# A decoder trunk re-laid with a transposed residual, streamed weights, and feed-forward work interleaved with attention

## The chip, the cores and the metric

The kernel runs on all eight cores of one Trainium2 chip, two dies of four cores each. Every core computes one batch element of 4,096 tokens, and no core waits for another. The metric is device time in microseconds of the slowest core. Some executions fall into a second, slower state: the cores of one die, or of both, show a lower granted TensorE clock (the share of full speed at which TensorE is let run) and take some per cent longer (in one run of the old kernel, experiment 9, 19,823.8 us at 0.881 on one die beside 18,640.3 at 0.958 on the other). I compare fast runs with fast runs. In the later jobs I compare single cores on a die that shows no lower clock in its records, and I call that an undisturbed die.

## The reference

Four layers. Each has a half-step SwiGLU feed-forward, a mixer, and a second half-step feed-forward. The model width is 1,024 and the hidden width 2,816. The mixer has 6 differential heads (two 32-wide score components, causal), 6 forgetting heads (causal with a learnt decay) and 4 dilated heads (an exact mixture of three windows, 2,048 tokens back at most).

```python
def reference(x, w_in, ...):
    for l in range(DEPTH):
        x = x + 0.5 * swiglu(rms_norm(x, g_ffn1[l]), w1_gate[l], w1_up[l], w1_down[l])
        x = x + hybrid_mixer(rms_norm(x, g_mix[l]), w_in[l], ...)   # diff | forgetting | dilated, then @ w_o
        x = x + 0.5 * swiglu(rms_norm(x, g_ffn2[l]), w2_gate[l], w2_up[l], w2_down[l])
    return rms_norm(x, g_final)
```

## The kernel before

It runs in stages, layer by layer over all 4,096 tokens: feed-forward, projections, attention, output projection, feed-forward. A small recording layer gives each engine its instructions and adds the semaphore waits that the buffers need (a semaphore is a counter by which one engine tells another, or itself, that work is done). Weights of a stage stay on chip while the stage runs. The stages in order, cut:

```python
    for idx, l in enumerate(layers):
        phase_ffn(c, g, w["w1_gate"][l], ...)
        phase_proj(c, g, sc, w["w_in"][l], ...)
        phase_attn(c, g, sc, w["w_o"][l], ...)
        phase_ffn(c, g, w["w2_gate"][l], ...)
    phase_final(...)
```

In attention the loop is a pipeline over items of one 128-key block and 512 queries. Scores are made two items ahead (`PRE`), and values are taken two items late (`LAG`), so TensorE, ScalarE (the exponential) and TensorE again work on different items:

```python
        LAG = ATT_LAG        # 2
        PRE = ATT_PRE        # 2
        for i in range(min(PRE, len(items))):
            emit_S(items[i])
        for i, it in enumerate(items):
            ...
            c.op("act", lambda e: e.activation(out=p[:, col0:w1], in_=sbk[:, col0:w1], func=AF.Exp,
                                               scale=hd["scale"]), reads=SBKS, writes=[P])
            ...
            if i + PRE < len(items):
                emit_S(items[i + PRE])
            if i >= LAG:
                emit_PV(i - LAG)
```

The softmax here doesn't subtract the row's maximum and nothing guards it: scores larger than these inputs give would overflow.

## Time and profile before

The median was 19,086.98 us over three runs (19,032.48 to 19,121.04). The profiled execution's slowest core took 18,680.2 us.

| stretch of layer 0 | us | what is busy in it |
|---|---|---|
| first feed-forward | 984 | TensorE |
| projections | 580 | TensorE |
| attention | 1,780 | TensorE and ScalarE both about 91% |
| output projection | 152 | TensorE |

These lines are from the page of the kernel before: its span, busy time by engine, three rows of the 40 equal slices (a digit is a busy share in tenths; PEclk is the granted TensorE clock in tenths of full speed), and the chain of work that ended last.

```profile
span 18680.2 us, 262548 instructions; the slowest of 8 cores (18600.2 to 18680.2 us)
PE 16574.1 (89%) x75072; PEld 7111.5 (38%) x75072; DVE 6278.7 (34%) x7537; ACT 9004.0 (48%) x17109; POOL 929.4 (5%) x716
PE   8978999799997899979898889997989898998794
ACT  2214999422222599932221269992222227998121
PEclk9989999999998999999999999999999999999997
PE 80%; DMA 8%; ACT 4%; DVE 4%; issue 3%; another core or an unknown queue 1%; SPq 1%; POOL 0%; ACTq 0%; DVEq 0%; POOLq 0%
```

The four runs of nines in the ScalarE row are the four attention stages. Between them ScalarE is nearly idle. A busy ScalarE in attention and a nearly idle one in the feed-forward is what the change sets out to even out.

The next lines are the table by stretch of the same kernel: the window, its length, then busy time and instruction count of TensorE matmuls, weight loads, VectorE, ScalarE and GpSimd, then granted clock, DMA share and GB/s.

```profile
core 3: us, PE busy (x) PEld busy (x) DVE busy (x) ACT busy (x) POOL busy (x), PEclk, DMA share, GB/s
119.00:1103.00 984.00, 889.05 (x4287) 409.79 (x4285) 208.83 (x292) 235.76 (x369) 6.12 (x7) 0.96 0.25 60
1103.00:1683.00 580.00, 526.93 (x2504) 236.97 (x2502) 193.53 (x259) 117.92 (x222) 114.10 (x82) 0.96 0.27 83
1690.00:3470.00 1780.00, 1624.70 (x6768) 632.54 (x6768) 885.48 (x953) 1613.72 (x3233) 76.23 (x55) 0.98 0.09 17
3470.00:3622.00 152.00, 121.20 (x512) 46.40 (x512) 43.72 (x64) 0.00 (x0) 0.00 (x0) 0.99 0.70 213
```

Attention keeps both engines at about 91% (1,624.70 and 1,613.72 of 1,780). If attention's matmuls could be mixed with the feed-forward's, ScalarE would no longer set its pace.

### The profile page before, as it was taken

How to read it: one execution, taken by the hardware profiler on the slowest of the kernel's cores; microseconds unless marked ns; L12 is line 12 of the kernel's file. 1: busy time of each engine (PE TensorE's matmuls, PEld its weight loads, DVE VectorE, ACT ScalarE, POOL GpSimd, SP SyncE). 2: the span in 40 equal slices, each digit the busy share in tenths (PEclk: the TensorE clock that was granted, in tenths of full speed). 3: DMA queues.
4: the chain of work that ended last, by engine and by line, in shares of the span. 5: the costliest groups of instructions: out<-in, count | busy, mean ns of one | idle time of the engine just before them, and what ended most of it. 6: DMA issues, size and time to landing. Idle time of an engine off the chain costs nothing.

```text
span 18680.2 us, 262548 instructions; the slowest of 8 cores (18600.2 to 18680.2 us)
## 1 busy us (share of the span) xinstructions
PE 16574.1 (89%) x75072; PEld 7111.5 (38%) x75072; DVE 6278.7 (34%) x7537; ACT 9004.0 (48%) x17109; POOL 929.4 (5%) x716
## 2 busy tenths in 40 slices
PE   8978999799997899979898889997989898998794
PEld 3433333244443333334444333333444343333341
DVE  2223444422222444532221344452222234445221
ACT  2214999422222599932221269992222227998121
POOL 0011000000001100000000110000000010000000
PEclk9989999999998999999999999999999999999997
DMA  4132001513114200151412310005141221001512
GB/s 87 52 84 64 10 13 23 116 59 84 55 50 95 53 12 12 23 124 54 88 55 61 88 40 12 16 20 132 55 90 55 67 85 29 10 17 34 126 55 92
DMA packets 854125, 1072.66 MB, mean 57 GB/s; under 512 B 339288, under 2 KB 529048, under 8 KB 844568
## 3 DMA queue, kind: packets, MB, share of 16 engines
q1 hardware_dynamic: 680240, 883.83, 15.8%
q0 software_dynamic: 172544, 172.03, 6.8%
q8 instruction: 710, 11.63, 0.3%
q14 instruction: 631, 5.17, 0.1%
HBM read 908.30 MB, written 319.36 MB: 66 GB/s over the span
## 4 chain that ended last, share of the span: by engine, by line
PE 80%; DMA 8%; ACT 4%; DVE 4%; issue 3%; another core or an unknown queue 1%; SPq 1%; POOL 0%; ACTq 0%; DVEq 0%; POOLq 0%
PE ps L832 16%; PE pp L295 13%; PE pp L299 13%; PE ps L327 12%; PE pp L766 12%; PE pp L520 4%; PE pp L528 3%; PE ps L562 2%; PE pp L761 2%; DMA out<-L3m_xr 1%; DMA fin_xt<-out 1%; DMA out<-L1m_xr 1%; PE pp L763 1%; DMA out<-L2m_xr 1%
## 5 line engine op out<-in xcount | busy, mean ns | idle before, releaser
L832 PE MATMUL ps<-L1m_pt,L1m_va 128*128 128x512 bf16 (+3 forms) x3072 | 1117.8, 364 | 35.4 <-DVE L1m_pt L886 16.4
L832 PE MATMUL ps<-L2m_pt,L2m_va 128*128 128x512 bf16 (+3 forms) x3072 | 1117.0, 364 | 32.2 <-DVE L2m_pt L886 15.5
L832 PE MATMUL ps<-L0m_pt,L0m_va 128*128 128x512 bf16 (+3 forms) x3072 | 1115.8, 363 | 32.6 <-DVE L0m_pt L886 16.4
L832 PE MATMUL ps<-L3m_pt,L3m_va 128*128 128x512 bf16 (+3 forms) x3072 | 1111.1, 362 | 32.7 <-DVE L3m_pt L886 16.4
L880 ACT ACTIVATE L1m_pt<-pp 128x512 bf16<-128x512 f32 (+3 forms) x2208 | 1043.0, 576 | 60.6 <-PE pp L763 22.5
L880 ACT ACTIVATE L2m_pt<-pp 128x512 bf16<-128x512 f32 (+3 forms) x2208 | 1043.0, 576 | 58.8 <-PE pp L763 21.6
L880 ACT ACTIVATE L0m_pt<-pp 128x512 bf16<-128x512 f32 (+3 forms) x2208 | 1043.4, 576 | 57.7 <-PE pp L763 20.3
L880 ACT ACTIVATE L3m_pt<-pp 128x512 bf16<-128x512 f32 (+3 forms) x2208 | 1042.8, 576 | 57.3 <-PE pp L763 20.1
L766 PE MATMUL pp<-L2m_qz,L2m_ks 128*128 128x512 bf16 (+3 forms) x1824 | 679.9, 373 | 55.6 <-ACT L2m_pt L880 55.5
L766 PE MATMUL pp<-L0m_qz,L0m_ks 128*128 128x512 bf16 (+3 forms) x1824 | 678.5, 373 | 56.2 <-ACT L0m_pt L880 55.8
L766 PE MATMUL pp<-L1m_qz,L1m_ks 128*128 128x512 bf16 (+3 forms) x1824 | 678.8, 373 | 55.7 <-ACT L1m_pt L880 55.5
L766 PE MATMUL pp<-L3m_qz,L3m_ks 128*128 128x512 bf16 (+3 forms) x1824 | 677.9, 372 | 55.7 <-ACT L3m_pt L880 55.5
L832 PEld LDWEIGHTS ps<-L1m_pt,L1m_va 128*128 128x128 bf16 x3072 | 295.3, 96 | 694.6 <-issue 643.3
L832 PEld LDWEIGHTS ps<-L2m_pt,L2m_va 128*128 128x128 bf16 x3072 | 295.1, 96 | 692.5 <-issue 640.0
L832 PEld LDWEIGHTS ps<-L0m_pt,L0m_va 128*128 128x128 bf16 x3072 | 295.2, 96 | 689.6 <-issue 638.2
L832 PEld LDWEIGHTS ps<-L3m_pt,L3m_va 128*128 128x128 bf16 x3072 | 294.7, 96 | 682.3 <-issue 628.8
L876 ACT ACTIVATE L0m_pt<-pp,L0m_bq 128x512 bf16<-128x512 f32 (+1 forms) x864 | 472.9, 905 | 40.3 <-DVE L0m_bq L734 34.3
L876 ACT ACTIVATE L1m_pt<-pp,L1m_bq 128x512 bf16<-128x512 f32 (+1 forms) x864 | 474.1, 884 | 36.5 <-DVE L1m_bq L734 25.7
L876 ACT ACTIVATE L2m_pt<-pp,L2m_bq 128x512 bf16<-128x512 f32 (+1 forms) x864 | 473.2, 904 | 36.2 <-DVE L2m_bq L734 29.3
L876 ACT ACTIVATE L3m_pt<-pp,L3m_bq 128x512 bf16<-128x512 f32 (+1 forms) x864 | 471.8, 909 | 32.7 <-DVE L3m_bq L734 27.8
L302 ACT ACTIVATE L0c_sg<-pp 128x512 f32<-128x512 f32 x176 | 105.1, 597 | 678.1 <-PE pp L295 669.8
L302 ACT ACTIVATE L1c_sg<-pp 128x512 f32<-128x512 f32 x176 | 105.1, 597 | 677.9 <-PE pp L295 677.6
(547 smaller groups left out, 29103.9 us busy)
## 6 DMA issues: line engine op xcount, KB each, us to landing
L0a_xt<-x SPq DMA_DIRECT2D x32, 512.0 KB, 4.0
L0a_xr<-x SPq DMA_DIRECT2D x64, 256.0 KB, 2.9
out<-L0a_xr SPq DMA_DIRECT2D x64, 256.0 KB, 2.3
L0p_xt<-out SPq DMA_DIRECT2D x32, 512.0 KB, 4.1
L0m_xr<-out SPq DMA_DIRECT2D x64, 256.0 KB, 3.9
out<-L0m_xr SPq DMA_DIRECT2D x64, 256.0 KB, 4.2
L0c_xt<-out SPq DMA_DIRECT2D x32, 512.0 KB, 3.9
L0c_xr<-out SPq DMA_DIRECT2D x64, 256.0 KB, 2.9
```

The source lines that it names most:

```text
L295: (lambda e, kc=kc: e.matmul(pg[:], wg[:, kc, fc * 128:(fc + 1) * 128], xnT[b][:, kc, :], start=(kc == 0), stop=(kc == 7)))
L299: (lambda e, kc=kc: e.matmul(pu[:], wu[:, kc, fc * 128:(fc + 1) * 128], xnT[b][:, kc, :], start=(kc == 0), stop=(kc == 7)))
L302: c.op("act", lambda e: e.activation(out=sg[fc % 2][:], in_=pg[:], func=AF.Silu), reads=[PG], writes=[SG[fc % 2]])
L327: (lambda e, fc=fc: e.matmul(py[:], hT[:, fc, tt * 128:(tt + 1) * 128], wd[:, fc, dh * 512:(dh + 1) * 512], start=(fc == 0), stop=(fc == N ...
L520: (lambda e, kc=kc: e.matmul(pa[:], wq[:, kc, col:col + 128], xnT[b][:, kc, :], start=(kc == 0), stop=(kc == 7)))
L528: (lambda e, kc=kc: e.matmul(pb_[:], wq[:, kc, rcol:rcol + 128], xnT[b][:, kc, :], start=(kc == 0), stop=(kc == 7)))
L562: (lambda e, kc=kc: e.matmul(pv[:], xnT[b][:, kc, tt * 128:(tt + 1) * 128], wv[:, kc, hf * 512:(hf + 1) * 512], start=(kc == 0), stop=(kc ...
L761: lambda e: e.matmul(sbk[:, col0:512], kt[0:K, kb * 128:(kb + 1) * 128], qt[0:K, q0 + col0:q0 + 512], start=True, stop=False),
L766: c.op("pe", lambda e: e.matmul(sbk[:, col0:512], kt[0:K, kb * 128:(kb + 1) * 128], qt[0:K, q0 + col0:q0 + 512], start=True, stop=True), r ...
L832: c.op("pe", lambda e: e.matmul(obk[:, col0:512], va[vs][:, kb, :], p[:, col0:512], start=it["first"], stop=it["last"]), reads=[P, VA[vs]] ...
L876: c.op("act", lambda e: e.activation(out=p[:, col0:512], in_=sbk[:, col0:512], func=AF.Exp, scale=hd["scale"], bias=bq[bi][:, kb:kb + 1]), ...
L880: c.op("act", lambda e: e.activation(out=p[:, col0:w1], in_=sbk[:, col0:w1], func=AF.Exp, scale=hd["scale"]), reads=SBKS, writes=[P])
```

## The change

The kernel is rewritten. Its parts:

- The residual is kept transposed (model width on partitions), so no activations are transposed, and the work goes in blocks of 1,024 tokens. Sixteen block-layers of attention (4 layers times 4 blocks) are numbered `a = 0..15`.
- All the work of a block that is not attention (output projection, second feed-forward, first feed-forward of the next layer, projections) is one long generator, which I call a **chain**. There are 20. Chain `a + 3` is to run during attention of block `a`.
- Weights stream in 0.5 MB units through a ring of six, once per block instead of once per layer.
- Differential scores use four 32-row tiles of the array at once; exponentials are 1,024 columns wide.
- Attention has PSUM banks 0 to 5. Chains have the two others. (PSUM is the memory that holds TensorE's results, used here as eight banks; copying a finished bank out is called an eviction.)

The core of the diff, cut. Everything in it is added; `...` marks cuts, and the comments after `#` are mine:

```diff
+    def filler_step(self, force=False):          # next piece of a chain: 8 matmuls of 512 columns, about 1.73 us
+        ...
+        r = next(self.fill_gen)
+        ...
+        self.remF -= r                           # chain work still to be handed out
+        return r

+        self.filler_init()                       # sets self.remF = 0.0
+        ...
+        self.fill_limit = n - 2                  # n = 4: the prologue runs chains 0, 1, 2
+        while self.filler_step() is not None:
+            pass
+        self.tlbanks = [6, 7]
+        pend = None
+        ui = 0
+        RES = 12.0
+        for a in range(L * n):
+            tgt = a + n - 1
+            self.fill_limit = tgt
+            self.remF += self.tl_cost(tgt)       # this block's chain work, in us
+            ...
+            def fill(t):
+                ...
+                budget += t * max(0.0, self.remF - RES) / max(remA, 1e-9)
+                while budget > 0 and self.gap <= 0:
+                    r = self.filler_step()
+                    ...
+                    budget -= r
+            for st in steps:
+                self.emit_S(st)
+                ct = cost(st)
+                fill(ct / 2)
+                if pend is not None:
+                    self.emit_PV(pend)           # values of the step before: one step late
+                pend = st
+                fill(ct / 2)
+                remA -= ct
```

So between the score matmuls and the value matmuls of a step some chain pieces are put in: `remF` is the chain work left, `remA` the attention steps left, and their ratio spreads the one evenly over the other. A second way in is forced: where attention needs something that an unfinished chain makes, it runs chain pieces until that is there.

```diff
+            if self.nch <= ch["i"] or self.nq <= hd["i"]:     # in emit_S: keys or queries not there yet
+                self.filler_step(True)
+    def need_wo(self, a):                                     # before an attention output is overwritten
+        while self.wo_done < a:
+            self.filler_step(True)
```

## The prediction

> **What bounds the kernel now.** It runs in stages. Busy time by stretch (layer 0): feed-forward about 984 us, PE 935 busy, clock 0.97 to 1.00; projection about 580, PE 523; attention 1780, with ScalarE busy 1614 (91%); output projection 152; the gaps between stages 34 to 90 us each, clock near 0.5. In the timeline the feed-forward's 128x512 matmuls come 0.216 us apart, so feed-forward and projection sit at the TensorE rate. In attention one 512-column exponential costs about 0.58 us per item and TensorE is held to that: 3072 items x 0.58 = 1780. The span is 18,680 us; the timed median is about 400 us above it.
>
> **What the change does.** Attention of one block shares TensorE with the feed-forward and projections of the block three ahead; ScalarE's 1.6 ms per layer should hide under matmuls.
>
> - Removed: the rotated-weight projections (640 matmuls per layer, 138 us, 550 in all), the transposes, stage gaps (about 250 us per layer), zero-padded scores. The differential scores become four K=32 row tiles at once. [...] no trace here shows it yet. [...]
> - TensorE work left, counted from the instruction order at 0.216 us per 512 columns: feed-forward 7,290, projections and output 1,870, attention 3,960, fp32 norm sums 90: about 13,200 us.
> - ScalarE: wide 1024-column exponentials (0.94 to 1.0 us, extrapolated from 0.28 to 0.61 us for 128 to 512 columns) total about 5,500; tanh 840, squares 500, copies and table loads (1.28 us each) 1,100: about 8,000. VectorE about 7,000.
> - Added: weights are streamed four times as often (0.5 MB per unit, every 6.9 us at worst). Before loads 17.3 MB in 117 us, twice that rate; it should hide.
>
> **What TensorE will still wait for** (estimates): 52 norms, each a serial chain of add, square, GpSimd add, fp32 matmul, Ln with table load, Exp, multiply: 8 to 9 us, partly filled: 400 us. The feed-forward filler has only two PSUM banks; a gate bank needs tanh (0.60) plus a VectorE op (0.69), about 1.7 us with semaphores, against 1.73 us of matmuls, and queues behind 1 us exponentials: 0.3 us per gate/up pair, 420 us. Projection evictions 150; single-buffered differential scores in the longest blocks 150; accumulator evictions 150; start and tail 60. Total about 1,330, so a span of 14,500 and, with the same 400 us offset, 14,900 us.
>
> **Chances.** Predicted 14,900 us, 8 in 10 within 14,100 to 16,200. Faster by over 2%: 0.97; within: 0.02; slower: 0.01.
>
> **What would show the steps right or wrong.** Page after: TensorE above 90% busy in nearly all slices, ScalarE 50 to 60%, DMA four tenths. Four row-tiled score matmuls start almost together. The chain of waits mainly TensorE, with waits on the evictions of the two filler banks and on the norm chain.
>
> **What would make it wrong.** A lower granted clock: [...] This case's trace disagrees so far: all eight cores hold 1.0 in the feed-forward. [...] Bank or queue waits larger than 0.3 us per pair: each 0.1 us costs 140 us.

Where the text is marked, passages are cut whose figures no trace or run had shown: the time of a group of four row tiles with the 900 us that tiles without overlap would add, and what I wrote of a lower clock's cause with a time of about 17,000 us worked out from it. The sum was 13,200 us of TensorE work plus 1,330 of waits, so a span of 14,500, and 14,900 with the offset. The cut time of a group is no separate term of it, and the record does not say what a group of row tiles counts for within the 3,960 us of attention. (With a group put down as one matmul of 0.216 us, the changed kernel's columns come to 13,157 us in the account below.) The 1.0 that all eight cores hold is read from 4,700 to 5,600 us of the kernel before, a feed-forward of layer 1, where each core's mean is 1.00; over the first feed-forward core 3 has 0.96, as in the table above.

## The result, and the profile after

| | median us | lowest to highest | runs |
|---|---|---|---|
| before | 19,060.32 | 19,032.48 to 19,121.04 | 4 |
| after | 20,717.72 | 20,527.38 to 20,831.25 | 4 |

The ratio of fast runs is 1.0847 (95% interval 1.0784 to 1.0909): the changed kernel is slower. The ratio is the mean time of one kernel's fast runs over that of the other's of the same rounds, so it is not quite the ratio of the two medians. I had predicted 14,900 us, faster with a chance of 0.97.

The same parts of the page, for the changed kernel:

```profile
span 20525.9 us, 227698 instructions; the slowest of 8 cores (20482.2 to 20525.9 us)
PE 16631.8 (81%) x68016; PEld 5945.0 (29%) x68016; DVE 6932.5 (34%) x10341; ACT 8106.0 (39%) x10325; POOL 2165.3 (11%) x2496
PE   6877788788897978778788787977978888777878
ACT  1133543633514153462441416256153232646361
PEclk9978799798798979879889897987987989796879
PE 63%; ACT 12%; issue 11%; DVE 7%; DMA 4%; POOL 2%; SPq 0%; ACTq 0%; DVEq 0%; POOLq 0%
```

I had expected TensorE above 90% in nearly all slices. It is mostly at seven or eight tenths. ScalarE is no longer in four lumps, but it still swings between 1 and 6 tenths, which an even mixture would not do. The clock row falls to 7 again and again, where the old kernel held 8 or 9 up to the last slice. TensorE's share of the last chain fell from 80% to 63%, and ScalarE, VectorE and "issue" took its place.

The table by stretch of one block (`a = 2`: differential, forgetting, dilated heads) on core 6 of the changed kernel:

```profile
core 6: us, PE busy (x) PEld busy (x) DVE busy (x) ACT busy (x) POOL busy (x), PEclk, DMA share, GB/s
2501.00:3530.00 1029.00, 855.23 (x3715) 306.14 (x3716) 326.01 (x486) 366.09 (x474) 129.77 (x151) 0.91 0.37 79
3530.00:3718.00 188.00, 143.43 (x581) 55.65 (x579) 40.16 (x49) 145.88 (x156) 1.04 (x1) 0.92 0.15 43
3718.00:3895.00 177.00, 141.99 (x325) 38.42 (x323) 79.62 (x130) 84.68 (x106) 0.00 (x0) 0.50 0.12 35
```

The dilated stretch runs at a granted clock of 0.50 from end to end. "PE busy 141.99 of 177" there doesn't mean that TensorE had much to do: while the clock records say 0.5, dense matmuls of 512 columns come 0.43 us apart in this trace in place of 0.216, and the columns of these matmuls at full clock would have filled 64 us, a share of 0.36. VectorE and ScalarE are busy less than half of it. GpSimd, which starts the weight loads for the chains, does nothing at all.

Where are the chain's matmuls? The same three stretches, restricted to the chains' first main matmul line (columns: window, length, matmuls, weight loads, clock, DMA share, GB/s):

```profile
2501.00:3530.00 1029.00, 418.53 (x1680) 162.44 (x1680) 0.91 0.37 79
3530.00:3718.00 188.00, 0.00 (x0) 0.00 (x0) 0.92 0.15 43
3718.00:3895.00 177.00, 0.00 (x0) 0.00 (x0) 0.50 0.12 35
```

All 1,680 of them are in the differential stretch; the forgetting and the dilated heads get none. It is so in every block: in the whole trace of core 6 no chain matmul stands between two matmuls of forgetting or dilated heads. The interleaving that the change is about doesn't happen in two of the three kinds of heads. And inside the differential stretch it comes in long bursts rather than evenly, as the account of the bookkeeping below shows.

### An account of the span

To see what TensorE's span is made of, I split every start-to-start interval of matmuls in the trace into three parts: the time that the columns need at full clock (0.2158 us for 512 columns, the spacing seen where matmuls run densely), the surplus that the granted clock explains, and the rest, a stall. This is my own computation from the trace's records, not a view of the profile. How a pause is shared between clock and stall depends on the rule: a recheck with another rule gave 1,958 and 5,265 for the changed kernel, with a sum within 25 us of the one below. A group of four row-tiled score matmuls is put down as one matmul; what it takes beyond that stands among the stalls.

```
us per core                       span   columns at  lower    stalls  before first and
                                         full clock  clock            after last matmul
predicted                       14,500     13,200        0     1,330  (in the stalls)
after, core 6                   20,526     13,157    1,762     5,483      123
reset, core 1 (experiment 1)    17,467     13,134      641     3,558      133
 + no self-wait, core 4         16,657     13,134      523     2,878      122
 + values two steps late, c. 1  16,330     13,132      485     2,579      134
```

The work was predicted well (13,200 against 13,157). What failed is everything between: stalls were 5,483 instead of 1,330, and the clock cost 1,762 where I had put nothing. The largest stalls after the change, with the same items after the fixes of the experiments:

```
us of stall                                          after   reset   +no self  +lag 2
value matmul after a score matmul (forg., dilated)   1,529     893       839      431
chain after chain, same kind of matmul               1,161     427       209      198
differential score after a value matmul              1,133     381       479      469
differential value after a differential value          565     550         8       (small)
differential value after a differential score          409     254       262      261
```

### The profile page after: what moved, and what is told of

It is laid out like the page before. It is cut to its first block, busy times and chain, and to the rows that moved or that the text cites. A ratio compares the mean times of both kernels' runs of the same rounds, so it can differ in the third digit from the quotient of the medians.

```text
span 20525.9 us, 227698 instructions; the slowest of 8 cores (20482.2 to 20525.9 us)
## 1 busy us (share of the span) xinstructions
PE 16631.8 (81%) x68016; PEld 5945.0 (29%) x68016; DVE 6932.5 (34%) x10341; ACT 8106.0 (39%) x10325; POOL 2165.3 (11%) x2496
## 4 chain that ended last, share of the span: by engine, by line
PE 63%; ACT 12%; issue 11%; DVE 7%; DMA 4%; POOL 2%; SPq 0%; ACTq 0%; DVEq 0%; POOLq 0%
PE ps L520 24%; PE ps L549 14%; PE ps L948 6%; PE ps L960 6%; ACT pt L893 6%; PE pp L911 5%; ACT pt L921 4%; PE pp L883 3%; PE pp L520 2%; DVE xn L505 2%; DMA s_vd<-hT 2%; DMA s_qf<-hT 2%; ACT pt L925 1%; PE ps L713 1%; PE pp L549 1%
## 5 line engine op out<-in xcount | busy, mean ns | idle before, releaser
L520 PE MATMUL ps<-xn,ring 128*128 128x512 bf16 x24216 | 5830.3, 393 | 376.9 <-ACT hT L687 118.7
L893 ACT ACTIVATE pt<-pp 128x1024 bf16<-128x1024 f32 (+3 forms) x3456 | 3100.6, 949 | 1425.1 <-PE pp L883 1420.8
L520 PEld LDWEIGHTS ps<-xn,ring 128*128 128x128 bf16 x24216 | 2327.9, 100 | 3775.5 <-issue 1430.3
L960 PE MATMUL ps<-pt,vr 128*128 128x512 bf16 (+3 forms) x5376 | 2040.6, 454 | 1091.3 <-DVE dd L982 393.6
L948 PE MATMUL ps<-pt,vr 128*128 128x512 bf16 (+3 forms) x6912 | 2307.9, 421 | 494.4 <-DVE dd L982 217.4
L549 PE MATMUL ps<-hT,ring 128*128 128x512 bf16 x10296 | 2378.4, 378 | 140.0 <-DVE t L585 0.2
L911 PE MATMUL pp<-qr,kr 66*128 66x512 bf16 (+3 forms) x5376 | 2083.5, 463 | 0.6
L921 ACT ACTIVATE pt<-pp,ckm 128x1024 bf16<-128x1024 f32 (+7 forms) x1920 | 1812.0, 964 | 570.9 <-PE pp L911 395.3
L549 PEld LDWEIGHTS ps<-hT,ring 128*128 128x128 bf16 x10296 | 937.4, 97 | 1577.7 <-issue 586.2
L984 DVE RECIPROCAL dd<-dd 128x128 f32<-128x128 f32 x1408 | 1338.7, 951 | 119.2 <-DVE dd L984 3.2
L960 PEld LDWEIGHTS ps<-pt,vr 128*128 128x128 bf16 x5376 | 539.3, 101 | 2711.3 <-issue 2634.7
L948 PEld LDWEIGHTS ps<-pt,vr 128*128 128x128 bf16 x6912 | 451.4, 99 | 1942.7 <-issue 1899.7
```

Source lines behind the costliest of these rows:

```text
L520: fns = [(lambda e, k=k: e.matmul(p[0:m, :] if m != 128 else p, w[:, woff + k * m:woff + (k + 1) * m], self.xn[:, k, b * 512:(b + 1) * 512 ...
L549: fns.append(lambda e, w=w, o=o, ap=ap, q=q: e.matmul(p, w[:, o:o + 128], ap, start=(q == 0), stop=(q == nblk - 1)))
L893: c.op("act", lambda e: e.activation(out=v3(p[:], c0, 512), in_=v3(self.pp[m][:], c0, 512), func=AF.Exp, scale=SCALE_D), reads=self.PS[2 * ...
L911: fns.append(lambda e, a0=a0, a1=a1, tri=tri: e.matmul(pp[:, a0:a1], kr[0:66, kc:kc + 128], qr[0:66, a0:a1], start=True, stop=not tri))
L921: c.op("act", lambda e: e.activation(out=p[:, lo:hi], in_=pp[:, lo:hi], func=AF.Exp, scale=1.0, bias=self.ckm[par][:, kb, hd["h"]:hd["h"] ...
L948: c.group("pe", [(lambda e, cc=cc: e.matmul(self.pst[cc][:, c0:512], va, p[:, cc * 512 + c0:(cc + 1) * 512], start=(st["first"] and m == 0 ...
```

## Experiments

Letters stand for theories where they are used: C is the wait of TensorE on its own semaphore, E is the single step between scores and values, G is that the half clock comes from too little TensorE work (a guess from the 0.50 at a share of 0.36 above; experiment 7 does not show it).

### The main theory: a counter that starts at minus 943.5

`remF` is meant to hold the chain work still to be handed out. The prologue runs chains 0 to 2 through the same `filler_step`, which subtracts each piece, but nothing was added for them. So the main loop starts with `remF` at minus the cost of three chains. Replaying the bookkeeping while the kernel is built (no chip needed) prints, for the first line of each kernel, `remF` as block 11's cost is added, and for the others how many us of chain work were forced and how many were spread:

```
after    a 11 remF before -400.9 adds 570.2
         -1 forced 0 free 943.5          (prologue)
          0 forced 0 free 0
          1 forced 342.1 free 0
          2 forced 506.3 free 63.9
         13 forced 570.2 free 0
         15 forced 255.7 free 483.8      (the rest, after the last attention)
reset    a 11 remF before 12.1 adds 570.2
          0 forced 0 free 300.7
          1 forced 0 free 572.0
          2 forced 0 free 570.2
         15 forced 0 free 524.0
```

Most blocks start from -400.9 and add 570.2. So `remF` is positive at first, but far too small, and the forced pieces soon use it up: of 570 us only 62 to 67 are spread. In blocks 0 and 1 and after block 12 it is never positive. There the budget is `t * max(0, negative)`, nothing. All the chain work then arrives by the forced way, in a burst when attention comes to a head whose keys or outputs are not ready. The rival was that the interleaving is sound and the two filler banks and their evictions make the stalls, as my prediction had it.

### Experiment 1: reset the counter

```diff
         self.tlbanks = [6, 7]
+        self.remF = 0.0
         pend = None
```

> One line: the account of filler time still to be placed (remF) is set to zero after the first three feed-forward chains, which had driven it to -943 us. Theory A (the schedule was never interleaved: with the account negative the budget is zero, and the chains run only where attention is forced to wait for them): filler now spreads over differential, forgetting and dilated heads; the granted clock rises from 0.86 to 0.97 or more, the time falls from 20,700 to about 14,500 to 15,600 us. Theory B (the loss is in the parts themselves: two PSUM banks for the chains, row tiles that do not overlap, weight streaming[...]): time stays within 3% of 20,700[...].

The result was correct. The first profiled execution had one die in the slow state:

```profile
die 0 (median of its cores): 17455.5 us, clock 0.934
die 1 (median of its cores): 18426.6 us, clock 0.859
```

In the seven runs (17,468.04 to 19,467.87) the undisturbed dies took 17,428 to 17,476 us. In one run both dies were undisturbed, and it took 17,468.04 us. The kernel before, in the same rounds, had no run without a slow die (19,521.27 to 20,557.94), so there is no ratio of fast runs; its one undisturbed die took 18,668 to 18,694. Theory A's numbers were missed all the same: the clock rose to 0.934 and not to 0.97, and the time did not come down to 15,600 us; experiments 3 and 4 go on from there. One added line is worth 20,526 - 17,467 = 3,058 us on a core: 1,925 of stalls and 1,121 of clock. On undisturbed cores the changed kernel goes from 9.9% slower than the old one (20,526 over 18,680) to 6.6% faster (17,452 over 18,681, middles of those ranges).

The same restriction to the chain's matmul line, same block, after the reset (differential, forgetting, dilated):

```profile
2846.00:3400.00 554.00, 197.23 (x776) 73.05 (x777) 0.94 0.35 76
3400.00:3705.00 305.00, 151.89 (x632) 61.33 (x631) 0.98 0.33 68
3705.00:3961.00 256.00, 73.83 (x272) 26.85 (x272) 0.89 0.47 118
```

776 + 632 + 272 = 1,680, the same matmuls, now spread. The whole block takes 554 + 305 + 256 = 1,115 us instead of 1,394. The dilated stretch holds more work, is longer, and runs at 0.89 instead of 0.50.

### Experiment 2: reset, but spread only in the first two layers

```diff
+        self.remF = 0.0
...
-                budget += t * max(0.0, self.remF - RES) / max(remA, 1e-9)
+                budget += (a < 8) * t * max(0.0, self.remF - RES) / max(remA, 1e-9)
```

> As e1_reset, but the budget is zero again from layer 2 on, so layers 0 and 1 interleave and layers 2 and 3 do not. Theory A: blocks of layers 0 and 1 take as long as in e1_reset, blocks of layers 2 and 3 as long as in the changed kernel (about 1,250 and 1,600 us for the second and fourth kind of block), and the time lies between the two, near 17,500 to 18,500 us. Theory B: no difference between the layers.

Correct; 20,042.85 us, with both dies on a lower clock (about 0.82 and 0.81), so its total says nothing (17,500 to 18,500 was expected) and only blocks of the same kernel may be compared. These are the three stretches of the fourth block of layer 1, with spreading, and of the fourth block of layer 2, without, on core 1, restricted to the chains' first main matmul line as before:

```profile
8859.00:9570.00 711.00, 248.61 (x880) 89.09 (x880) 0.85 0.33 74
9570.00:9958.00 388.00, 126.34 (x528) 51.04 (x528) 0.94 0.28 61
9958.00:10206.00 248.00, 85.78 (x272) 30.03 (x272) 0.75 0.42 110
13229.00:14422.00 1193.00, 400.75 (x1680) 159.93 (x1680) 0.87 0.33 73
14422.00:14669.00 247.00, 0.00 (x0) 0.00 (x0) 0.94 0.14 42
14669.00:14847.00 178.00, 0.00 (x0) 0.00 (x0) 0.51 0.11 33
```

The first block took 711 + 388 + 248 = 1,347 us, the second 1,193 + 247 + 178 = 1,618 us (1,250 and 1,600 were expected). On the other cores the pairs lie between 1,354 and 1,421, and between 1,618 and 1,718. One kernel thus shows both behaviours, and the switch between them is the spreading alone. This also speaks against a slow chip or a slow state as the cause.

### Experiment 3: leave out TensorE's waits on its own semaphore

The recording layer makes an instruction wait for the last writer of each bank it writes. Where a second group accumulates into the same bank, the last writer is TensorE itself, so TensorE waits until its own earlier group is done (0.32 us each time in a differential value product, see below). All 68,016 matmul records on core 6 of the changed kernel start in the order of the program, and the results of experiments 3, 4 and 8 stayed right without the wait: it guards nothing here.

```diff
     def wait(self, e, s, v):
+        if e == "pe" and s == "c_pe":
+            return
```

> e1_reset, and TensorE no longer waits on its own semaphore (it runs in order [...]). Theory C (in the interleaved kernel a part of what is left is TensorE waiting for its own drain between two groups that accumulate into one bank: 550 us between the two halves of a differential value product, some of the 430 us inside the chains): span of an undisturbed core falls from 17,460 by 500 to 900 us, and the 0.32 us pauses between those halves go. Rival D (those pauses are row-tile switching or late weights): no change beyond 1%.

Correct (on top of the reset). Undisturbed dies: 16,657 to 16,707 us; one run without a slow die, 16,692.09. That is 811 us less than the reset (17,467 to 16,657). The reset was measured on another chip; the kernel before took 18,609 to 18,694 us on undisturbed dies of that one and 18,585 to 18,739 on this one, so I take the two as alike. One step shows it. The timeline of the changed kernel (start, duration, engine, source line, operation, count), four value matmuls of a differential step:

```profile
4300.52 0.40 PE L883 MATMUL pp<-qr,kr 32*128 32x512 bf16 x4 [1.06 <-ACT pt L893]
4300.85 1.35 PE L948 MATMUL ps<-pt,vr 128*128 128x512 bf16 x4
```

and the same four without the self-wait:

```profile
4201.46 1.03 PE L950 MATMUL ps<-pt,vr 128*128 128x512 bf16 x4
```

1.35 - 1.03 = 0.32 us, 1,737 times in the changed kernel: 565 us in the account, and 8 us with the wait left out. The chain's long accumulations gained as well (chain after chain, 427 to 209). The first line shows something else: four 32-row score matmuls of 512 columns took 0.40 us from start to end together, where a single matmul of that size is shown with 0.38. They run at once. But the next matmul starts 0.33 us after the first of the four, not 0.216: more on this below.

### Experiment 4: values two steps late

```diff
-        pend = None
+        pends = deque()
...
-                if pend is not None:
-                    self.emit_PV(pend)
-                pend = st
+                if len(pends) >= 2:
+                    self.emit_PV(pends.popleft())
+                pends.append(st)
```

> e3_noself, and the value products follow their scores by two steps instead of one. Theory E (TensorE's 890 us of waits at the forgetting and dilated value products are for the mask and the exponential of the step just before): they halve, span falls by a further 300 to 500 us. Rival F (they are for the eviction of the two accumulators): less than 150 us.

Correct (on top of both fixes). All six runs were slow ones (16,775.72 to 18,441.7); in four of them one die was undisturbed, at 16,329 to 16,387 us (in the profiled one, two of its cores show 0.8125 for 154 us). That is 327 us less than experiment 3, and the stall of values behind scores fell from 839 to 431. What it cures can be read in the dilated stretch of the changed kernel. This is its timeline (start, duration, engine, line, operation; in brackets the idle time before it and what ended that), with lines in between cut:

```profile
3821.96 1.02 ACT L925 ACTIVATE pt<-pp 128x1024 bf16<-128x1024 f32 x1 [0.90 <-DVE pt L928]
...
3822.14 1.01 PE L960 MATMUL ps<-pt,vr 128*128 128x512 bf16 x2 [0.33 <-DVE pt L928]
...
3822.94 1.06 PE L911 MATMUL pp<-qr,kr 66*128 66x512 bf16 x2
...
3824.16 1.02 ACT L925 ACTIVATE pt<-pp 128x1024 bf16<-128x1024 f32 x1 [1.17 <-PE pp L911]
...
3825.28 0.69 DVE L928 TENSOR_TENSOR pt<-pt,wt 128x1024 bf16<-128x1024 bf16 x1 [1.50 <-ACT pt L925]
3826.16 1.02 ACT L925 ACTIVATE pt<-pp 128x1024 bf16<-128x1024 f32 x1 [0.98 <-PE pp L911]
...
3826.23 1.01 PE L960 MATMUL ps<-pt,vr 128*128 128x512 bf16 x2 [0.22 <-PE pp L911]
```

Follow one step: values of an earlier step at 3822.14, then this step's scores at 3822.94, the exponential at 3824.16, the mask product at 3825.28, its values at 3826.23. That is 4.09 us for two steps, and no engine is full: it is a round of handovers. With chain pieces put in between, TensorE has something to do in the meantime; with a second step under way, the round counts for less. The old kernel had that second step (`LAG` 2, `PRE` 2), and its dilated heads held a clock of 0.99; that the second step is the reason was not tested on it.

This version is the best that I ran. On one chip and in the same rounds its undisturbed dies took about 16,350 us, the kernel before's 18,585 to 18,739: about 12% less. All six of its runs were below all seven of the kernel before (19,790.87 to 20,718.78, also all slow ones).

### Experiment 5: load a quarter of each weight unit

After the first six, only a quarter of each unit is loaded, so the result is wrong (relative error 1.16), but the program is otherwise that of experiment 1.

```diff
+        w = 2048 if self.uld <= RING else 512
-        self.c.dma("pool", ..., self.ring[:, s * 2048:(s + 1) * 2048], self.w["w_units"][l, u], ...)
+        self.c.dma("pool", ..., self.ring[:, s * 2048:s * 2048 + w], self.w["w_units"][l, u][:, 0:w], ...)
```

> e1_reset with three quarters of the weight stream left out after the first six units (wrong result on purpose; the ring keeps old weights). The prediction said that the stream hides: then the span of an undisturbed core stays within 1.5% of 17,460 us and the stalls of TensorE within 200 us of 3,560. If the stream crowds out other transfers, the span falls by more than 500 us.

Its undisturbed die took 17,259 to 17,278 us, 1.1% less than experiment 1 on the other chip, with stalls of 3,409 against 3,558. In its two other runs both dies were slow. So the fourfold weight traffic is nearly hidden, as predicted, and is not where the time went. This run differs from experiment 1 in its chip and in the data of its weights too; what of the 1.1% belongs to the traffic was not separated.

### Experiment 6: the reset again, on the other chip

> The same kernel as e1_reset, as the reference of this chip: 17,460 us on an undisturbed die, more on a die whose clock is limited; stalls of TensorE near 3,560 us in either.

19,267.8 us, both dies on a lower clock (0.81 and 0.82). On core 4 the account gives 2,514 us to the clock, some 1,860 of them at 0.8125, and 3,194 to stalls, where I had expected 3,560 on any clock. This run is no measure of the reset: it shows what the lower clock cost this kernel.

### Experiment 7: dilated scores twice, in the changed kernel

```diff
+            if kind == "dil":
+                fns = fns + fns
             c.group("pe", fns, reads=[KR, QR, self.CONST], writes=PPS)
```

> The changed kernel without the reset of the counter; every score matmul of the dilated heads is issued twice in a row into the same banks (the second overwrites the first with the same values, so the result stays right). In the changed kernel the dilated stretches have no chain work and TensorE has about 64 us of full-clock work in 177 us (share 0.36) at a granted clock of 0.50 to 0.51; in the stretch that was looked at ScalarE and VectorE are busy less than half of it. Theory G (the half clock is granted because TensorE has little work there): the share of issued work rises to about 0.5 to 0.55, the granted clock in the dilated stretches rises clearly above 0.51 (0.7 or more), and the stretch does not get longer than 190 us although it holds about 30 us more work at full clock; the whole run stays within 1.5% of the changed kernel on cores of an undisturbed die. Rival (the half clock belongs to the data or to the shape of the dilated heads' matmuls): the clock stays at 0.50 and the stretches lengthen by about twice the added work, 50 to 70 us each, so the run by some 600 to 850 us.

Correct. The dilated stretch of block 2 on two cores of the undisturbed die, core 1 and core 3:

```profile
3753.00:3948.00 195.00, 169.19 (x483) 57.17 (x481) 79.89 (x130) 84.86 (x107) 0.01 (x1) 0.62 0.11 32
3756.00:3967.00 211.00, 196.01 (x486) 63.12 (x483) 79.50 (x130) 84.67 (x106) 0.00 (x0) 0.50 0.10 29
```

Neither expectation was met. On core 1 the stretch got 18 us longer (177 to 195) for 32 us more work at full clock, and the clock rose from 0.50 to 0.62, not to 0.7 or more. On core 3 the same stretch stayed at 0.50 and got 34 us longer, so 0.62 is no fair sample. Over the dilated stretches of core 1 (blocks 0 to 14) the share of work rose from 0.35 to 0.45 and the mean clock only from 0.51 to 0.54; on the die's other cores the mean was 0.54 to 0.56. Core 1's whole time rose by 301 us (20,827 against 20,526), at the upper edge of what theory G allowed and well under the rival's 600 to 850. In the two other runs one die was undisturbed again, with the same times (20,796 to 20,856 us).

So this experiment does not show that the amount of work sets the clock. What speaks for it is the forgetting stretch of the changed kernel's block 2: matmuls of the same shapes, a share of 0.58 (columns at full clock over the stretch) and a clock of 0.92; and the 0.89 of experiment 1, where the dilated heads have chain work between them and the share is 0.71. How much work is enough isn't settled, and the share alone does not fix the clock: the kernel before ran its dilated heads at 0.99 with a share of 0.65.

### Experiment 8: no self-wait, without the reset

```diff
     def wait(self, e, s, v):
+        if e == "pe" and s == "c_pe":
+            return
```

> The changed kernel without the reset of the counter; only TensorE's waits on its own semaphore are left out, which was worth 790 us when the counter was reset. In the changed kernel 1,737 stalls of a value matmul after a value matmul in the differential heads take 565 us. Theory: those go (to about 10 us), and the run loses 400 to 700 us on an undisturbed die, to 19,800 to 20,150 us: the run stays slower than before, so the self-wait alone does not explain why the prediction failed. Rival (the self-wait is hidden, or it is the main cause): the run stays within 150 us of 20,500, or falls below 19,000.

Correct. Undisturbed die: 19,788 to 19,810 us, 716 to 738 less than the changed kernel's core, at the lower edge of what I had written and a little more than the 400 to 700 us. The stall of 565 us fell to 14, chain after chain from 1,161 to 717, but scores that follow a value matmul rose from 1,133 to 1,460: part of what the wait took had only stood in front of another. In the second run both dies were on a lower clock (0.79). The kernel stays slower than before. So the self-wait is a real cost, but not the reason for the wrong prediction.

### Experiment 9: the kernel before, with its clock records

No edit.

> The kernel before, unchanged, with its clock records. Where a die is on the lower clock, its records should show 0.8125 in it as the reset kernel's did, so the slow state is not made by the change: about 20,500 us on such a die and 18,600 to 18,750 us on a die without. [...]

```profile
die 0 (median of its cores): 19823.8 us, clock 0.881
die 1 (median of its cores): 18640.3 us, clock 0.958
```

On core 0 the clock records say 0.8125 for 8,528 us; on core 5, of the other die, never. So this die ran at a lower clock for a part of the run and took 19,824 us, not the 20,500 expected. Other runs of it took up to 20,660.38. The slow state is thus no product of the change.

## Why the prediction was wrong, point by point

- **"Attention of one block shares TensorE with the feed-forward and projections of the block three ahead; ScalarE's 1.6 ms per layer should hide under matmuls."** This is the step that failed. I took the intent for the order. The order of instructions, which needs no chip, shows all of a block's chain matmuls between differential heads, and a replay of the counter says why: it starts at -943.5, so the budget is zero or soon used up. Experiments 1 and 2 show it: one added line takes 3,058 us off a core, and switching the spreading off after layer 1 brings the old blocks back within the same run.
- **"Total about 1,330" of stalls.** Mis-sized: 5,483 in the changed kernel, and still 3,558 with the counter right. Terms that the list didn't have at all: values that wait for an exponential only one step back (839 before experiment 4, 431 after), and TensorE waiting on itself (811 us by experiment 3). I had read the waits of the recording layer as harmless where an engine waits on its own work.
- **The clock.** I had feared a lower clock, for a reason that no trace showed, and put nothing down for one in the sum. The changed kernel lost 1,762 us to a clock of 0.5. Of 5,716 us at that clock on core 6, 2,085 are in the dilated stretches, which hold it almost throughout; 2,864 are in the differential ones, where the chains' bursts are, and I have not shown why the clock falls there. In the changed kernel's scored trace core 6 shows only 0.5 and 1.0. The slow state appears as 0.8125 in later runs, the old kernel's included: my "this case's trace disagrees so far" held for the profiled runs of the scored comparison only.
- **"With the same 400 us offset."** There is no constant offset. In every run whose cores are listed, the time is the slowest core's span plus 1 to 2 us (20,527.38 against 20,525.9). Where the old kernel's later runs were above 18,680, a die was in the slow state. The first three runs list no cores, so for them this is the likely reading, not a shown one.
- **Right: the size of the work.** TensorE columns 13,157 (predicted 13,200), ScalarE 8,106.0 (about 8,000), VectorE 6,932.5 (about 7,000).
- **Row tiles: the overlap was right, its size was not.** The four score matmuls of a group start within 0.013 us of one another. But in 1,536 groups on core 6 (1,344 of four times 512 columns, 192 of two times 512 and two times 384) the next matmul never starts less than 0.32 us after the first of the four, with 0.33 at the median, where single matmuls of 512 columns come 0.216 us apart: 4 x 0.216 / 0.33 = 2.6 times. My own figure for a group came from no trace and was lower. What holds the next matmul back was not tested. My estimate from these figures: 1,536 x (0.33 - 0.216) = 175 us of the stalls above.
- **Right: wide exponentials and the weight stream.** 1,024 columns took 1.02 us (predicted 0.94 to 1.0, so just above), and 1.11 in the forgetting heads. The stream is worth 1.1% at most (experiment 5).

Of the 6,026 us between the predicted span and the changed kernel's, the counter took 3,058, the self-wait 811 and the single step 327. What is left, 1,830 us, between the best version (16,330 us on a core) and the predicted span of 14,500: 485 of clock, and 2,579 + 134 of stalls and ends against 1,330. Of those, 469 are scores that wait for the one set of differential score banks (my estimate was 150), 431 values behind scores, and the rest is in many small items. No run here takes these apart further.

## What to carry to other kernels

Before costing an overlap, check in the order of instructions that the work really stands where the design wants it; a counter in the scheduler is part of the kernel, and its state at the start of the loop deserves a line of output. When a large change moves time the wrong way, split the span into needed columns, clock and stalls: a stretch at half clock that looks busy may hold little work (142 us busy and 64 us of work here). TensorE's waits on itself (811 us by experiment 3) and a software pipeline with a single step of slack (327 us by experiment 4) each cost hundreds of microseconds here and could be seen in one timeline window.

## What the traces show of the clock and of table loads

- In the dilated stretch of the changed kernel (177 us at 0.50) no pause between matmuls is longer than 2.64 us and matmuls are recorded for 142 of the 177 us; the share of work at full clock was 0.36. The forgetting stretch just before, with a share of 0.58, had 0.92. Which amount of work, or which spacing, keeps the full clock stays open: in other kernels 0.49 went with 0.50 and with 0.62, 0.71 with 0.89, and 0.65 with 0.99.
- In the profiled run of the kernel before, no clock record of any of the eight cores is below 1.0 except 0.5 (1,515 to 1,633 us of it on each core), and all eight ran dense matmuls (888 to 892 us busy in the 900 us from 4,700 to 5,600); in another run of it core 0 had 0.8125 for 8,528 us and core 5, of the other die, none. What brings the 0.8125 on is not shown by these runs.
- These lines of ScalarE's timeline in the kernel before show 1.28 us for an ACT_TABLE_LOAD:

```profile
4063.24 0.19 ACT L167 ACTIVATION_READ_ACCUMULATOR L0c_junk<-L0c_xt 128x1 f32 x1
4063.51 1.28 ACT L169 ACT_TABLE_LOAD   x1
4064.81 0.30 ACT L169 ACTIVATE L0c_rs<-L0c_ss,eps_norm 128x1 f32<-128x1 f32 x1
```

  The load starts 0.08 us after the operation ahead of it ends, and the next operation starts 0.02 us after the load: with both gaps it takes about 1.4 us there. In all 465 loads on that core the next operation starts within 0.02 us of the load's end.
